# Cross attention by a product of the query weight and the memory keys: one change to a decoder step on one core

## The chip, the cores and the metric

The kernel runs on one core of a Trainium2 chip. The metric is the device time of one launch in microseconds (us). The core has five engines that run side by side and wait for each other through semaphores: TensorE (PE; its weight loads are shown as PEld), VectorE (DVE), ScalarE (ACT), GpSimd (POOL) and SyncE (SP). Sixteen DMA engines move data between HBM and the on-chip memory; transfers are issued from the queues of SP, ACT and POOL. Every engine executes its instructions in a fixed order. Before the change the median of three runs is 1817.83 us (1816.76 to 1819.05).

## The reference

One step of a decoder layer on two groups that share the weights: a prompt of 1024 rows of width 1024, and a sample group of 8 rows with long caches. Per layer: self-attention heads with a forget gate beside spatial gating heads, an output projection, then cross attention into 256 memory tokens, then a gated feed-forward network with a short convolution. The change concerns the cross attention of the prompt:

```python
def memory_kv(mem, g_mem, w_ck, w_cv):
    mn = rmsnorm(mem, g_mem)
    mk = (mn @ w_ck).reshape(B, M, MEM_HEADS, MEM_HEAD_DIM)     # 256 x 4 x 256, an output too
    mv = (mn @ w_cv).reshape(B, M, MEM_HEADS, MEM_HEAD_DIM)     # an output too

def cross_attend(xn, mk, mv, w_cq, w_co):
    q = (xn @ w_cq).reshape(B, T, MEM_HEADS, MEM_HEAD_DIM).astype(mk.dtype)
    s = jnp.einsum('bqhd,bmhd->bhqm', q, mk).astype(jnp.float32) * (MEM_HEAD_DIM ** -0.5)
    p = jax.nn.softmax(s, axis=-1).astype(mv.dtype)
    o = jnp.einsum('bhqm,bmhd->bqhd', p, mv).reshape(B, T, MEM_HEADS * MEM_HEAD_DIM)
    return (o @ w_co).astype(xn.dtype)
```

There are 4 heads of 256 columns, so queries, keys of all heads and values are each 1024 wide. All inputs are float32. The scores of a head are `xn @ (w_cq_h @ mk_h.T)`: the inner matrix does not depend on the rows.

## The kernel before

The prompt goes through in two halves of 512 rows. `prompt()` is a generator that chains the stages: `p1` (input projections of all rows), `attention(0)` (self-attention of the first half) mixed with a filler, `attention(1)`, and then for each half an output projection (`out_proj` with w_o), `cross`, which ends in `out_proj` with w_co, and `ffn`. The filler is `pmem()`, which computes the memory keys and values from `mem`, w_ck and w_cv, writes them to the outputs `o_mk` and `o_mv` and leaves them there to be read again, followed by the gating of the first half.

Every stage yields a planned time after each piece of work. Two planners use it. `mix(main, bg, ratio)` runs a filler beside a stage: it hands out filler worth `ratio` times the stage's planned time (`MIXR` for attention and `pmem`). And `build` itself runs the sample group beside everything: for each amount `PACE[phase]` of planned time it takes one step of the generator `sample()`. A step of its main part, `decode`, gathers one tile of 1 MB of cached keys (L1407), multiplies it by the query and reduces it on VectorE (L1423, L1427), and 18 steps later gathers the matching tile of values (L1469) and multiplies it on TensorE (L1475). `NKV` = 4 tiles (`kv`) are shared by these gathers. After 148 steps comes `sample_rest`, which is TensorE work on weights loaded once more. The final order on each engine is made by a scheduler from these instructions; a gather's place in the order hangs on the planned times.

Matmuls with weights are made of three products (`gemm3`, L272 to L274): each float32 operand is split into a high part of reduced precision (`h`, by a copy on ScalarE, L235 or L238) and a rest (`l`, by a subtraction on VectorE, L236 or L239), and high x high, high x low and low x high are accumulated. `wload` loads a weight tile of 128 x 1024 (512 KB) from the SP queue into one of `WR` = 4 buffers `wr` and splits it into `wh` and `wl`. The matmuls named fp32 below are made on unsplit float32 operands; the trace shows each of them as two instructions.

`norm_T` transposes the rows of a half 256 at a time, splits them with the gain and calls `first` when a group of 256 is there. `cross` before the change:

- loads keys and values of two heads (`fetch`), loads w_cq in two halves of 512 columns, and projects queries: for each of 8 blocks of 128 query columns, 24 products with 512 rows as the moving operand (`products`). The first block is computed in two groups of 256 rows from `norm_T`. The result is copied out of PSUM.
- `keys(h)`: four transposes bring a head's keys into place (L1153), a copy leaves PSUM (L1157).
- `weigh(h)`: for each of the four 128-row tiles two fp32 products of 256 columns (L1170), the maximum over two tiles on VectorE (L1172), the scaled exponentials (L1178) and the scaling by the reciprocal of the sum (L1183) on ScalarE.
- `turned(h)`: transposes of the weights (L1190) and their copy (L1191).
- `gather(h)`: the fp32 product with the values (L1198) and the split of the result for the output projection.

Other lines in the quoted rows: L640 the gating's mixing matmuls, L1106 the transposes in `norm_T`, L1055 to L1075 the matmuls of `out_proj`, L1545 the loads of `sample_rest`.

## Time and profile before

| | |
|---|---|
| median of three runs | 1817.83 us (1816.76 to 1819.05) |
| the profiled execution | 1820.56 us |
| its span, first to last instruction | 1818.4 us |
| mean granted TensorE clock | 0.986 |
| HBM traffic | 495.47 MB read, 23.93 MB written |
| DMA | 521.06 MB, mean 287 GB/s |

The page of the profile gives the busy time of each engine, 40 slices of the span, the DMA queues, the chain of work that ended last, and the costliest groups of instructions. A row of a group reads: line, engine, operation, written tile <- read tiles, shapes, count | busy time in us, mean length of one in ns | idle time of the engine just before, and what ended it. A row of a stretch reads: the stretch, its length, then per engine the busy time and the number of instructions, the granted clock, the share of time that the 16 DMA engines were busy, and GB/s. In the chain and in the timeline a row begins with the start in us from the span's start and the length.

By line numbers the stages stand as follows: `p1` up to 239 us, `attention(0)` with `pmem` and the first gating to about 349, `attention(1)` to 488, the first half's `out_proj` (w_o) to 548, `cross` without its output projection to 652, that projection to 707, `ffn` to 1107, the same for the second half to 1183, 1295, 1351 and 1818.

### The profile page before, as it was taken

What the parts mean: (1) busy time and instruction counts of PE and PEld (TensorE: products, weight loads), DVE (VectorE), ACT (ScalarE), POOL (GpSimd) and SP (SyncE); (2) the same over time, 40 slices, a digit from 0 to 9 for tenths busy, and PEclk for the clock granted to TensorE, in tenths of its full rate; (3) what the DMA queues carried; (4) which work ended last, traced back from release to release, by engine and by line L of the source; (5) the groups of instructions that cost most, each with busy time, mean ns of one, the idle gap of its engine ahead of it and who ended that gap; (6) DMA issues with size and microseconds to landing.
All of it is one profiled execution on the core that took longest, in us unless ns stands there. A gap on an engine that the chain in (4) does not pass through costs nothing.

```text
span 1818.4 us, 25090 instructions
## 1 busy us (share of the span) xinstructions
PE 1745.0 (96%) x9637; PEld 1294.9 (71%) x9637; DVE 1397.5 (77%) x1729; ACT 734.4 (40%) x1378; POOL 510.0 (28%) x461
## 2 busy tenths in 40 slices
PE   8999999888998999999999999989899999999997
PEld 5887776656676767777777776766576778767775
DVE  4689668888788877999989899898875549845344
ACT  6332365455643544433333244235353324332332
POOL 1252334332133432223332333334222111011110
PEclk9999999899999999999999999989999999999999
DMA  8886889777696986679878779988787777568982
GB/s 295 306 297 231 302 297 329 242 266 224 219 398 257 342 310 260 257 285 340 316 279 311 271 306 340 381 300 324 290 309 290 267 268 265 179 266 289 359 314 82
DMA packets 157074, 521.06 MB, mean 287 GB/s; under 512 B 20874, under 2 KB 40842, under 8 KB 124186
## 3 DMA queue, kind: packets, MB, share of 16 engines
q0 software_dynamic: 57168, 341.14, 49.5%
q1 hardware_dynamic: 92874, 165.73, 26.4%
q10 hardware_dynamic: 6912, 12.59, 1.8%
q8 instruction: 76, 1.25, 0.3%
q14 instruction: 44, 0.36, 0.1%
HBM read 495.47 MB, written 23.93 MB: 286 GB/s over the span
## 4 chain that ended last, share of the span: by engine, by line
PE 72%; DMA 10%; issue 7%; DVE 6%; ACT 2%; POOL 2%; SPq 0%; POOLq 0%; DVEq 0%; ACTq 0%
PE ba L272 11%; PE ba L274 11%; PE ba L273 11%; PE bb L272 5%; PE bb L273 5%; PE bb L274 5%; PE dv L1475 5%; DMA kv<-cache_k,io 3%; DMA wr<-w_in 2%; DMA kv<-cache_v,io 1%; PE dv L321 1%; PE dv L1751 1%; PE ba L1056 1%; PE ba L1055 1%; PE ba L1057 1%
## 5 line engine op out<-in xcount | busy, mean ns | idle before, releaser
L235 ACT ACTIVATE wh<-wr 128x1024 fp32r<-128x1024 f32 (+2 forms) x220 | 228.9, 1044 | 489.2 <-PE ba L273 156.0
L236 DVE TENSOR_TENSOR wl<-wr,wh 128x1024 fp32r<-128x1024 f32 (+2 forms) x220 | 262.5, 1200 | 175.6 <-PE ba L274 65.7
L1407 POOL DMA_INDIRECT kv<-cache_k,io x128 | 205.6, 1606 | 551.2 <-DVE s L1427 318.9
L1423 DVE TENSOR_TENSOR kv<-kv,d 128x1024 f32<-128x1024 f32 (+1 forms) x156 | 258.0, 1681 | 35.1 <-DMA kv<-cache_k,io 35.1
L1427 DVE TENSOR_REDUCE s<-kv 128x16 f32<-128x1024 f32 (+1 forms) x156 | 258.2, 1674 | 0.1
L1469 POOL DMA_INDIRECT kv<-cache_v,io x128 | 165.3, 1291 | 282.8 <-PE dv L1475 191.8
L272 PE MATMUL ba<-u,wh 128*128 128x512 f32 (+1 forms) x560 | 220.3, 395 | 1.7 <-ACT u L238 1.7
L273 PE MATMUL ba<-u,wh 128*128 128x512 f32 (+1 forms) x560 | 220.2, 393 | 1.7 <-DVE u L239 1.5
L274 PE MATMUL ba<-u,wl 128*128 128x512 f32 (+1 forms) x560 | 219.5, 393 | 0.0
L272 PE MATMUL ba<-wh,u 128*128 128x512 f32 (+1 forms) x495 | 186.9, 379 | 0.9 <-ACT u L235 0.9
L273 PE MATMUL ba<-wl,u 128*128 128x512 f32 (+1 forms) x495 | 185.4, 375 | 1.2 <-DVE wl L236 1.2
L274 PE MATMUL ba<-wh,u 128*128 128x512 f32 (+1 forms) x495 | 183.8, 376 | 0.0
L272 PEld LDWEIGHTS ba<-u,wh 128*128 128x128 f32 x560 | 106.8, 191 | 30.6 <-issue 5.6
L273 PE MATMUL bb<-u,wh 128*128 128x512 f32 (+1 forms) x304 | 119.4, 393 | 9.2 <-DVE u L239 9.2
L274 PEld LDWEIGHTS ba<-u,wl 128*128 128x128 f32 x560 | 106.9, 191 | 29.1 <-issue 6.1
L273 PEld LDWEIGHTS ba<-u,wh 128*128 128x128 f32 x560 | 106.7, 191 | 27.5 <-issue 2.7
L1475 PE MATMUL dv<-kv,s 128*32 128x512 f32 x1024 | 124.2, 598 | 1.8 <-DMA kv<-cache_v,io 1.8
L272 PE MATMUL bb<-u,wh 128*128 128x512 f32 (+1 forms) x304 | 119.4, 393 | 0.0
L274 PE MATMUL bb<-u,wl 128*128 128x512 f32 (+1 forms) x304 | 118.6, 390 | 0.0
L272 PEld LDWEIGHTS ba<-wh,u 128*128 128x128 f32 x495 | 93.0, 188 | 26.0 <-issue 6.9
L274 PEld LDWEIGHTS ba<-wh,u 128*128 128x128 f32 x495 | 92.8, 188 | 21.5 <-issue 3.7
L273 PEld LDWEIGHTS ba<-wl,u 128*128 128x128 f32 x495 | 93.1, 188 | 19.7 <-DVE wl L236 1.9
(425 smaller groups left out, 3255.9 us busy)
## 6 DMA issues: line engine op xcount, KB each, us to landing
wr<-w_up SPq DMA_DIRECT2D x88, 512.0 KB
kv<-w_up POOLq DMA_DIRECT2D x22, 1024.0 KB, 8.0
wr<-w_down SPq DMA_DIRECT2D x40, 512.0 KB
kv<-w_down POOLq DMA_DIRECT2D x11, 1024.0 KB, 8.5
wr<-w_in SPq DMA_DIRECT2D x16, 512.0 KB
wr<-w_o SPq DMA_DIRECT2D x16, 512.0 KB
wr<-w_cq SPq DMA_DIRECT2D x16, 512.0 KB
wr<-w_co SPq DMA_DIRECT2D x16, 512.0 KB
```

What stands on the lines that cost most here:

```text
L235: nc.scalar.activation(h, src, AF.Copy)
L236: nc.vector.tensor_tensor(l, src, h.bitcast(F32), op=ALU.subtract)
L272: mmul(out, sh, mh, start=(i == 0), stop=False)
L273: mmul(out, sh, ml, start=False, stop=False)
L274: mmul(out, sl, mh, start=False, stop=(i == n - 1))
L321: mmul(ps[32 * j : 32 * j + 32, :w], xT[:, k, :] if nk == 8 else xT[:, k * 8 : k * 8 + 32], raw[:, q, j * w : (j + 1) * w], start=(k == 0) ...
L1055: mmul(pss[i], mh[k][:, tb], wh, start=(k == korder[0]), stop=False)
L1407: nc.gpsimd.indirect_dma_start(kv, None, a["cache_k"], off(kidx[:, b, ch : ch + 1]))
L1423: nc.vector.tensor_tensor(kvv[:, i : i + m, :], kvv[:, i : i + m, :], qb.unsqueeze(1).broadcast_to((P, m, 512)), op=ALU.mult)
L1427: nc.vector.tensor_reduce(s[:, ch * 4 + i : ch * 4 + i + m, :].rearrange("p k h -> p (k h)"), kvv[:, i : i + m, :].rearrange("p k (h d) -> ...
L1469: nc.gpsimd.indirect_dma_start(kv, None, a["cache_v"], off(kidx[:, b, ch : ch + 1]))
L1475: mmul(dv[32 * j : 32 * j + 32, :], s[:, ch * 4 : ch * 4 + 4, :].rearrange("p k h -> p (k h)"), kvv[:, j, :], start=(ch == 1), stop=(ch == ...
```

## The change

The product of the query weight with the keys, `wk = w_cq_h @ mk_h.T` for all four heads (1024 x 1024), is made once, in `pmem`, and kept in HBM (`wk_d`). `cross` then takes the scores of two heads and 128 rows from one dense product of the normalised rows with `wk`, 512 columns wide, and does the softmax for each such tile.

- `pmem` first projects the keys, reads each half of them back (`fetched`), turns and splits them (`turned`: 8 transposes and 2 splits a half), then for each head and each half of the model's columns loads a tile of the transposed query weight (`w_cqT`, a new input prepared with the other layouts) and makes 12 products of 256 columns for each of two PSUM tiles, copies them out on ScalarE and writes them to `wk_d` from the ACT queue (`into_queries`). The values are projected after that.
- `cross` loads `wk_d` where it loaded w_cq. The rows are now the stationary operand (`scores`), and `norm_T` may get a generator from `first`, so that the first two row tiles are scored, and yield, when their rows are there. `weigh` takes one tile of 128 rows x 2 heads, `turned` transposes it four tiles later. The key loads, the key transposes and the fp32 scores are gone; the values are gathered as before.
- `out_proj` gets its left operand by a function `of(k, i)` and may run something after a k step (`between`): the last transposes and the gathers of heads 2 and 3 are run there.
- `MIXR` is 1.5 instead of 1.0.

```diff
-MIXR = 1.0
+MIXR = 1.5
...
+    wk_d = dram.tile([D, D], F32, tag="wk_d", name="wk_d")
...
+        def turned(t):
+
+            h2, l2 = U([P, 2, 512], F32R), U([P, 2, 512], F32R)
+            for j in range(2):
+                tr = TR()
+                for dd in range(2):
+                    for mt in range(2):
+                        nc.tensor.transpose(
+                            tr[:, dd * 256 + mt * P : dd * 256 + (mt + 1) * P],
+                            t[:, mt, j * 256 + dd * P : j * 256 + (dd + 1) * P],
+                            ident,
+                        )
+                split(tr, h2[:, j, :], l2[:, j, :])
+                yield 0.5
+            return h2, l2
+
+        def into_queries(n, h2, l2):
+
+            for j in range(2):
+                for c in range(2):
+                    w = wload(wpair(a["w_cqT"], n * 2 + j, c * 512, 512), 1024)
+                    for q in range(2):
+                        ps = MM()
+                        for i in range(2):
+                            mb = slice((q * 2 + i) * P, (q * 2 + i + 1) * P)
+                            gemm3(
+                                ps[:, i * 256 : (i + 1) * 256],
+                                [
+                                    (w[0][:, d_, mb], w[1][:, d_, mb], h2[:, j, d_ * 256 : d_ * 256 + 256], l2[:, j, d_ * 256 : d_ * 256 + 256])
+                                    for d_ in range(2)
+                                ],
+                            )
+                        t = T2()
+                        nc.scalar.activation(t, ps, AF.Copy)
+                        r0, c0 = c * 512 + q * 256, (n * 2 + j) * 256
+                        nc.scalar.dma_start(
+                            wk_d[r0 : r0 + 256, c0 : c0 + 256].rearrange("(a p) k -> p a k", p=P), t.rearrange("p (a k) -> p a k", k=256)
+                        )
+                    yield 2.9
+
+        raws = []
+        for n in range(2):
+            yield from project(a["w_ck"], mk_d, n)
+            raws.append(fetched(mk_d, n))
+        for n in range(2):
+            h2, l2 = yield from turned(raws[n])
+            yield from into_queries(n, h2, l2)
+        for n in range(2):
+            yield from project(a["w_cv"], mv_d, n)
...
     def cross(xt, sq):
...
+        loaded = lambda n: [wload(wpair(wk_d, kk, n * 512, 512), 1024) for kk in range(4)]
...
+        def scores(i, hs, ls):
+            ps, tb = MM(), slice(i * P, (i + 1) * P)
+            gemm3(
+                ps,
+                [(hs[k][:, tb], ls[k][:, tb], ws[k // 2][0][:, k % 2, :], ws[k // 2][1][:, k % 2, :]) for k in range(8)],
+            )
+            return ps
+
+        def weigh(n, i, ps):
+
+            sv = ps.rearrange("p (j m) -> p j m", m=256)
+            mx, bs, l, r = (sm([P, 2], tag, 2) for tag in ("cmx", "cbs", "cl", "cr"))
+            nc.vector.tensor_reduce(mx, sv, axis=AX.X, op=ALU.max, negate=True)
+            nc.scalar.activation(bs, mx, AF.Copy, scale=rq[:, i : i + 1])
+            pp = T2().rearrange("p (j m) -> p j m", m=256)
+            for j in range(2):
+                nc.scalar.activation(
+                    pp[:, j, :], sv[:, j, :], AF.Exp, bias=bs[:, j : j + 1], scale=rq[:, i : i + 1], accum_out=l[:, j : j + 1]
+                )
+            nc.vector.reciprocal(r, l)
+            for j in range(2):
+                nc.scalar.activation(pp[:, j, :], pp[:, j, :], AF.Copy, scale=r[:, j : j + 1])
+            weights.append((n, i, pp))
...
+        def first(hs, ls, c):
+            i0 = c.start // P
+            r = rows_rstd(sq, i0, i0 + 2)
+            nc.vector.tensor_scalar(rq[:, i0 : i0 + 2], r, 1.0 / 16, None, op0=ALU.mult)
+            for i in (i0, i0 + 1):
+                weigh(0, i, scores(i, hs, ls))
                 yield 5.2
...
+        hs, ls = yield from norm_T(xt, G_CROSS, first)
+        ws = loaded(1)
+        for i in range(4):
+            ps = scores(i, hs, ls)
+            turned()
+            weigh(1, i, ps)
+            yield 5.6
+            if i == 1:
+                fetch(0)
+                fetch(1)
+        turned()
+        for h in range(2):
+            gather(h)
+            turned()
+            fetch(h + 2)
+            yield 3.8
...
+        yield from out_proj(a["w_co"], of, xt, ys=ys, between={0: turned, 1: partial(gather, 2), 2: partial(gather, 3)})
```

195 lines of the change are left out of this document (61 added, 134 removed).

## The prediction

> **What bounds the kernel now.** I read the page first, then the busy table by stretches, then single groups in the two stretches that the change rewrites, then start times of neighbouring matmuls. The page:
>
> ```profile
> span 1818.4 us, 25090 instructions
> PE 1745.0 (96%) x9637; PEld 1294.9 (71%) x9637; DVE 1397.5 (77%) x1729; ACT 734.4 (40%) x1378; POOL 510.0 (28%) x461
> PE 72%; DMA 10%; issue 7%; DVE 6%; ACT 2%; POOL 2%; SPq 0%; POOLq 0%; DVEq 0%; ACTq 0%
> ```
>
> TensorE is busy nearly all the time and carries 72% of the chain that ended last, so what counts is TensorE work and the holes in it. The stretches that matter (length; then busy time and instructions of PE, PEld, DVE, ACT, POOL; granted clock; DMA share; GB/s):
>
> ```profile
> 239.00:349.00 110.00, 101.77 (x550) 77.57 (x549) 83.61 (x144) 61.18 (x131) 40.81 (x52) 0.99 0.84 302
> 548.00:652.00 104.00, 97.36 (x502) 69.52 (x500) 88.00 (x114) 53.18 (x125) 37.52 (x25) 0.97 0.85 318
> 1183.00:1295.00 112.00, 98.67 (x499) 69.30 (x499) 95.00 (x113) 52.72 (x122) 41.71 (x29) 0.94 0.83 306
> 1351.00:1380.00 29.00, 27.38 (x165) 21.01 (x164) 17.84 (x32) 17.80 (x38) 4.09 (x6) 0.94 0.49 193
> 1380.00:1410.00 30.00, 30.00 (x160) 19.10 (x159) 14.64 (x21) 9.70 (x17) 7.36 (x8) 1.00 0.94 344
> 1410.00:1440.00 30.00, 30.00 (x152) 20.07 (x152) 16.19 (x23) 10.82 (x18) 5.72 (x7) 1.00 0.95 348
> ```
>
> 239 to 349 is the first half's self-attention with the memory projections as filler; 548 to 652 and 1183 to 1295 are the two halves' cross attention up to its output projection; from 1351 on stands the second half's FFN. The cross stretches are the ones where TensorE falls short of the stretch and the clock dips.
>
> A busy matmul is not its cost, since matmuls overlap. Cost per matmul is the distance between starts: first and last of 29 products with 260 columns, then of 21 with 512.
>
> ```profile
> 83.79 0.28 PE L272 MATMUL ba<-wh,u 128*128 128x260 f32 x1
> ...
> 87.16 0.28 PE L273 MATMUL bb<-wl,u 128*128 128x260 f32 x1
> ...
> 299.64 0.39 PE L272 MATMUL bb<-wh,u 128*128 128x512 f32 x1
> ...
> 304.24 0.40 PE L274 MATMUL bb<-wh,u 128*128 128x512 f32 x1
> ```
>
> 3.37 us over 28 steps is 0.120 us, 4.60 over 20 is 0.230.
>
> Now both cross stretches together (216 us), by source line in this order: L1170 fp32 scores, L1153 key transposes, L1198 value gather, L1475 decode's value products, L1190 and L1106 transposes, L640 gating.
>
> ```profile
> sum 216.00, PE 32.07 PEld 24.65; mean PE 16.03 PEld 12.33
> sum 216.00, PE 5.00 PEld 3.97; mean PE 2.50 PEld 1.98
> sum 216.00, PE 24.47 PEld 10.15; mean PE 12.23 PEld 5.07
> sum 216.00, PE 25.01 PEld 5.42; mean PE 12.51 PEld 2.71
> sum 216.00, PE 8.57 PEld 7.26; mean PE 4.28 PEld 3.63
> sum 216.00, PE 8.80 PEld 6.96; mean PE 4.40 PEld 3.48
> sum 216.00, PE 2.21 PEld 2.17; mean PE 1.11 PEld 1.08
> ```
>
> These give 106.1 us. The query projection is 168 products of 512 columns and 48 of 256 per half: 336 x 0.230 + 96 x 0.120 = 88.8. Together 194.9; the other 21.1 us of the two stretches are stalls. Which:
>
> ```profile
> L273 PE MATMUL bb<-u,wh 128*128 128x256 f32 x16 | 5.8, 362 | 3.2 <-DVE u L239 3.2
> L1170 PE MATMUL ba<-t,u 128*128 128x256 f32 x40 | 9.6, 387 | 0.7 <-ACT t L1157 0.7
> L273 PE MATMUL bb<-u,wh 128*128 128x256 f32 x16 | 6.0, 376 | 6.0 <-DVE u L239 6.0
> L1170 PE MATMUL ba<-t,u 128*128 128x256 f32 x56 | 13.2, 384 | 1.9 <-ACT t L1157 1.9
> L1170 PE MATMUL bb<-t,u 128*128 128x256 f32 x8 | 3.6, 636 | 4.2 <-DVE u L236 4.2
> ```
>
> The first two rows are of the first half, the others of the second: 9.2 us wait for VectorE's split of the normalised rows (L239), 6.8 us stand before the fp32 scores. Named: 16.0 us.
>
> **The change, term by term.**
>
> *TensorE work.* Removed in both halves: scores and key transposes, 32.07 + 5.00 = 37.1 us. The projection by w_cq becomes the product with wk_d: 192 products of 512 columns a half, 2 x 192 x 0.230 = 88.3 for 88.8, nothing. Softmax transposes and gather keep their counts. Added once, in pmem: 192 products of 256 columns x 0.120 (nearest row: 260 columns) = 23.0, and 16 transposes at 5.00/32 = 0.16, 2.5. TensorE is full around them, so both lie on the path. Net 25.5 - 37.1 = -11.6 us.
>
> *Stalls in cross.* In after, each k step of the first stage has two tiles of 512 columns (6 x 0.230 = 1.4 us) behind each split where before had 3 x 0.120 = 0.36, so L239's 9.2 us can go; the scores with their 6.8 us are gone. In their place comes a longer softmax chain per tile (maximum, two exponentials, reciprocal, two scalings, transposes), which the order covers by the four next score tiles, 22 us. Bounds: 16.0 gained to 0 (other waits replace them). Decode still holds VectorE for 88 and 95 us of these stretches, so I take half: -8.
>
> *The attention stretch (239 to 349).* It gets the 25.5 us of TensorE work, and on the queues: SP issues eight w_cqT loads and two read-backs of the memory keys, ACT sixteen writes of wk_d. Two things can be late. First, the read-back: the key write and the read must land before the transposes, and attention's matmuls queue behind these on TensorE.
>
> ```profile
> kv<-cache_k,io POOLq DMA_INDIRECT x128, 8.5
> q1 hardware_dynamic: 92874, 165.73, 26.4%
> ```
>
> With 8.5 us each (the nearest landing) 17.0 are needed; the next column half's two tiles cover 48 x 0.230 = 11.0, attention's steps between them more. So 0 to 6.0. Second, traffic: 4 MB read, 4 MB written, 1 MB read back, and two decode steps that by the yields and PACE fall into this stretch (10 instead of 8), 2 MB each: 13 MB, at 302 GB/s 43 us. Free are 0.16 x 110 = 17.6 plus 25.5 of new length, 43.1: an even match. The writes go in 1 KB pieces; at q1's mean packet (0.264 x 1818.4 x 16 / 92874 = 0.083 us) 4096 of them take 21 us of all engines, where 4 MB at 302 GB/s take 13, so 8 may stick out. Bounds 0 to 14, I take 4: the read-back is the nearer case, and part of its cover is certain.
>
> *VectorE and ScalarE there.* Eight weight splits, four key splits, two decode steps:
>
> ```profile
> L236 DVE TENSOR_TENSOR wl<-wr,wh 128x1024 fp32r<-128x1024 f32 x208 | 252.3, 1219 | 154.5 <-PE ba L274 65.7 <-issue 25.1 <-PE bb L274 16.4
> L1427 DVE TENSOR_REDUCE s<-kv 128x32 f32<-128x2048 f32 x68 | 154.1, 2274 | 0.1
> ```
>
> 8 x 1.22 + 4 x 0.6 (half the columns) + 2 x 2 x 2.27 (a step's product taken as long as its reduction) = 21.2 us on VectorE, which has 26 us free before the stretch is lengthened: hidden. ScalarE has 49 us free for the same splits, sixteen copies out of PSUM and sixteen issues: hidden. If this cover were gone, the splits that feed the new products would add their 12 us.
>
> *Edits at nothing.* The reads of wk_d take the place of those of w_cq on the same queue, with the same size and the same splits. SP loses eight 256 KB loads of keys. Passing `of` instead of lists issues nothing; `between` moves the last softmax transposes and two heads' gathers among the output projection's matmuls, where they cost what they cost before, and covers their own chain. MIXR 1.5 hands out the longer filler faster, so that it still ends with attention.
>
> *Decode displaced.* Cross yields 20 units of planned time less per half at the same PACE. Following the yields: 19 steps for 21 in the first half's middle, 22 for 25 in the second's, two more in attention, and 22 instead of 18 left when the second FFN begins; the last key steps now fall there. That is 4 value and 2 key tiles of 1 MB: 6 MB at 348 GB/s, 17 us. The DMA engines are free for 0.51 x 29 + 0.06 x 60 = 18 us there: 0 to 17. If the slots (NKV = 4) fill late, what is late next is VectorE's key products and, queued behind them, the splits that the FFN's matmuls wait for. I take 4. Sample's last product comes nearer to the end, but the prompt's still ends last.
>
> *Sum.* -11.6 - 8 + 4 + 4 = -11.6 us. The span of 1818.4 becomes 1806.8. The profiled execution took 1820.56, 2.2 outside its span; the median of the runs is 1817.83, 2.7 below that execution, so in its terms I expect 1806.2, say 1806 us.
>
> **Rivals.**
>
> *Slower: decode moves instead of shrinking.* Place: cross and the front of the second FFN. For it speak two links of the chain of waits within the second cross stretch:
>
> ```profile
> 1226.57 10.73 DMA kv<-cache_k,io
> 1261.66 13.70 DMA kv<-cache_k,io
> ```
>
> There key gathers, not matmuls, hold the chain. Then no stall goes, and the displaced 6 MB cost their whole 17 us: -11.6 + 0 + 4 + 17 = +9.4, 1827 us. It decides as soon as the FFN's front costs over 7.6 us with no stall gained. Against it: DMA is at 0.49 just there.
>
> *Less gain: the attention stretch.* Read-back and small writes cost their whole 14: -11.6 - 8 + 14 + 4 = -1.6, 1816 us. For it the even balance of traffic, against it the many steps of attention between.
>
> *More gain.* All 16.0 us of stalls go and nothing new comes: -27.6, 1790 us.
>
> *Weight loads bound.* Each new product loads its own weights. If loads, not starts, add up, the removed loads are 24.65 + 3.97 = 28.6 us and the added 192 x 0.189 + 16 x 0.124 = 38.3:
>
> ```profile
> L272 PEld LDWEIGHTS ba<-wh,u 128*128 128x128 f32 x74 | 14.0, 189 | 0.0
> 66.00:109.00 43.00, 43.00 (x355) 42.15 (x353) 43.00 (x29) 12.48 (x22) 15.66 (x8) 1.00 0.77 275
> ```
>
> So +9.7 in place of -11.6, 1828 us with the other terms as taken. The last row speaks against it: 353 loads in 42.15 us are 0.119 each, though one lasts 0.189; they overlap too. The Trainium skill, "Perfetto Trace Analysis", section "Identifying the Most-Contended Engine", has this as a rule: matmul busy time is a bad measure of headroom, the summed time of weight loads a good one. By that rule the change adds TensorE load; by the row, loads at this shape can be summed to more than the wall.
>
> **How the numbers follow.** Chances: my forecast 0.45 (own range 1798 to 1814), more gain 0.09, decode moved 0.22, attention stretch 0.18, loads 0.06. A change of 0.2% (3.6 us) is about what a measurement of this kernel tells from none. Faster: 0.45 + 0.09 + 0.10 of the attention case = 0.64; same: 0.05 of it; slower: 0.22 + 0.06 + its last 0.03 = 0.31. The range goes from the full gain, 1790, to the slower cases with a few more us of the attention stretch's 14, 1832.
>
> **What the profile after would show.** Right: fp32 matmuls of 256 columns gone; 192 of 256 columns in attention starting 0.12 us apart; the two cross stretches together some 167 us instead of 216 (37 of work, 8 of stalls, five decode steps at 25.01/26); attention some 30 us longer. Wrong: matmuls waiting for a DMA of o_mk or for VectorE behind key gathers at the FFN's front, cross stretches together above 175 us, or 0.19 us between the new products.

## The result and the profile after

The changed kernel takes 1837.99 us in the median of five runs (1832.35 to 1841.27), the kernel before 1817.83 beside it (1815.47 to 1822.79): ratio 1.0101, 95% interval 1.0076 to 1.0127. It is about 1% slower, where 1806 was forecast. The profiled execution took 1834.17 us; of its page:

```profile
PE 1744.2 (95%) x9637; PEld 1290.1 (70%) x9637; DVE 1411.0 (77%) x1755; ACT 746.5 (41%) x1386; POOL 496.0 (27%) x463
PE 63%; DVE 9%; DMA 3%; issue 2%; ACT 2%; POOL 1%; DVEq 0%; POOLq 0%; ACTq 0%
```

TensorE is busy as long as before (1745.0 us), though by the prediction's count it has 11.6 us less to do, and its share of the chain that ended last falls from 72 to 63%, VectorE's rises from 6 to 9%. Busy time is time, not work: the granted clock is lower, as the view by cores has it after and before,

```profile
core 0: 1832.4 us, clock 0.980
```
```profile
core 0: 1818.4 us, clock 0.986
```

The mean covers idle time too. Counted by the clock records of the traces over TensorE's busy time alone, 53.4 us stood at half the clock after and 41.0 before, so 6.2 us were lost in this way, over half of the work saved. TensorE's holes, the span less its busy time, grew from 73.4 to 88.2 us, about as much as the span, which is 14.0 us longer. (By the medians the loss is 20.2; the profiled execution is among the changed kernel's shorter ones.) Where, the busy table by stages tells (columns as before); the kernel before first: attention, the first FFN, and the second FFN in two parts.

```profile
239.00:497.00 258.00, 231.17 (x1435) 167.22 (x1434) 206.04 (x359) 153.37 (x335) 86.97 (x114) 0.97 0.75 257
707.00:1135.00 428.00, 422.16 (x2013) 314.98 (x2012) 394.63 (x382) 162.31 (x264) 127.78 (x89) 0.99 0.80 300
1351.00:1391.00 40.00, 38.38 (x220) 28.67 (x219) 23.98 (x41) 22.03 (x45) 6.78 (x8) 0.96 0.61 228
1391.00:1818.00 427.00, 417.16 (x2760) 311.11 (x2758) 242.71 (x363) 135.52 (x242) 64.96 (x93) 1.00 0.71 259
```

and the kernel after: attention; cross attention and its output projection; the first FFN; the second cross attention and its projection; the front of the second FFN and its rest.

```profile
239.00:538.00 299.00, 264.70 (x1670) 195.52 (x1669) 231.22 (x387) 176.75 (x370) 92.06 (x116) 0.95 0.76 267
587.00:660.00 73.00, 66.33 (x329) 47.40 (x328) 57.84 (x86) 41.26 (x104) 18.58 (x15) 0.98 0.69 257
660.00:724.00 64.00, 63.95 (x300) 43.59 (x299) 57.80 (x66) 21.03 (x40) 22.49 (x17) 1.00 0.90 345
724.00:1160.00 436.00, 427.09 (x2041) 319.18 (x2040) 405.07 (x394) 163.57 (x266) 132.58 (x94) 0.98 0.80 300
1207.00:1285.00 78.00, 71.56 (x353) 48.18 (x350) 63.25 (x89) 42.67 (x102) 20.86 (x19) 0.98 0.75 280
1285.00:1344.00 59.00, 59.00 (x271) 41.19 (x268) 54.08 (x57) 20.42 (x39) 23.48 (x18) 1.00 0.87 337
1344.00:1384.00 40.00, 31.12 (x170) 23.64 (x168) 31.40 (x39) 17.79 (x36) 13.55 (x10) 0.87 0.69 267
1384.00:1832.00 448.00, 434.40 (x2856) 319.19 (x2855) 259.25 (x385) 146.71 (x256) 75.23 (x103) 0.99 0.73 270
```

The next table has the stages of every run in us, from one profiled execution each. Attention is counted from 239 us to the first matmul of the w_o projection; the cross stages, with their output projection w_co, and the FFNs are cut at the first transpose of each `norm_T` and the first matmul of the second w_o projection. The two w_o projections stand between these columns. The expectations quoted below count attention only to its own last work, 249 us before and 287 after. The ratio is to the kernel before, with its 95% interval.

| run | ratio | attention | cross, w_co 1 | FFN 1 | cross, w_co 2 | FFN 2 |
|---|---|---|---|---|---|---|
| before | 1 | 258.1 | 159.1 | 428.6 | 168.2 | 467.6 |
| after | 1.0101 (1.0076 to 1.0127) | 298.8 | 137.6 | 436.1 | 136.4 | 488.9 |
| keys_only | 1.0205 (1.0163 to 1.0246) | 298.6 | 161.6 | 427.3 | 162.9 | 463.1 |
| unwritten | 1.0051 (1.0033 to 1.0069) | 293.7 | 138.3 | 436.6 | 136.7 | 487.7 |
| slots | 1.0080 (1.0059 to 1.0101) | 298.8 | 137.7 | 437.6 | 128.1 | 490.0 |
| pace | 1.0118 (1.0092 to 1.0144) | 302.5 | 137.7 | 449.2 | 138.3 | 477.4 |
| thin_before | 0.9286 (0.9270 to 0.9301) | 235.5 | 150.3 | 387.1 | 136.3 | 449.5 |
| thin_after | 0.9081 (0.9062 to 0.9100) | 256.1 | 116.7 | 386.1 | 115.1 | 450.0 |
| gate | 1.0087 (1.0064 to 1.0111) | 300.5 | 141.7 | 439.2 | 136.1 | 486.5 |
| hold | 1.0047 (1.0032 to 1.0062) | 302.0 | 135.4 | 435.1 | 128.5 | 489.5 |
| hold_slots | 1.0070 (1.0048 to 1.0091) | 301.2 | 135.0 | 433.8 | 128.6 | 488.6 |
| hs_att | 1.0153 (1.0136 to 1.0170) | 298.8 | 131.9 | 442.7 | 129.5 | 498.7 |
| hs_ffn | 1.0151 (1.0122 to 1.0179) | 301.1 | 135.6 | 453.3 | 136.6 | 478.9 |
| hs_mix1 | 1.0133 (1.0116 to 1.0150) | 300.0 | 133.6 | 439.8 | 129.4 | 502.9 |
| after_light | 1.0153 (1.0119 to 1.0186) | 296.6 | 133.1 | 433.7 | 134.1 | 507.5 |
| before_light | 1.0108 (1.0083 to 1.0132) | 256.3 | 163.1 | 426.5 | 165.8 | 474.7 |
| hs_light | 1.0182 (1.0160 to 1.0205) | 299.2 | 129.8 | 434.0 | 135.4 | 514.9 |
| hs_light2 | 1.0155 (1.0128 to 1.0181) | 286.5 | 129.1 | 426.7 | 137.9 | 516.9 |
| hs_mid1a | 1.0066 (1.0041 to 1.0090) | 304.2 | 135.4 | 432.8 | 131.1 | 491.9 |
| hs_mid1b | 1.0060 (1.0035 to 1.0086) | 302.7 | 135.2 | 434.0 | 131.4 | 495.1 |

Five of these runs (`after`, `keys_only`, `pace`, `gate`, `hold`) have the same order of instructions in attention on every computing engine, but for a few missing records, and five others (`slots`, `hold_slots`, `hs_ffn`, `hs_mid1a`, `hs_mid1b`) share another. The first five took 298.6 to 302.5 us there, the others 298.8 to 304.2: a difference under some 5 us in attention, read from one execution each, tells little. In the second FFN, `after`, `slots` and `unwritten`, nearly the same in order, lie within 2.3 us.

From before to after: attention +40.7, the cross stages -53.3, the FFNs +28.8, the two w_o projections -2.2; together the span's +14.0. Part of it is decode that changed places. Its value products (L1475 before, L1497 after) in the two cross stages and in the two FFNs, before:

```profile
sum 327.00, PE 38.69 PEld 8.24; mean PE 19.34 PEld 4.12
sum 895.00, PE 57.71 PEld 12.52; mean PE 28.86 PEld 6.26
```

and after:

```profile
sum 274.00, PE 30.52 PEld 6.42; mean PE 15.26 PEld 3.21
sum 924.00, PE 64.95 PEld 14.19; mean PE 32.48 PEld 7.09
```

So, with the prediction's figures for the work, the cross stages lost 37.1 of work, 8.2 of moved products and 8.0 of stalls. The FFNs gained 7.2 of moved products and 21.6 of something else, attention 25.5 of work, 1.9 of two more decode steps and 13.3 of something else. The two remainders, 34.9 us, are what the experiments are about. They are nearly all holes and low clock: TensorE's holes grew from 26.8 to 34.3 us in attention and from 17.3 to 31.4 in the FFNs, and its busy time at half the clock by 8.2 and 13.0 us, half of which is lost; that is 11.6 of the 13.3 and 20.6 of the 21.6. Key steps of the decode, counted as reduced tiles (L1427 before, L1449 after): cross stages 17 and 20 before, 13 and 15 after; FFNs 41 and 0 before, 43.5 and 5 after.

The largest single place is the second FFN's front. In 20 us TensorE is busy 12.75 after, 18.38 before:

```profile
1344.00:1364.00 20.00, 12.75 (x75) 9.85 (x73) 17.20 (x23) 10.29 (x24) 9.84 (x6) 0.74 0.76 301
```
```profile
1351.00:1371.00 20.00, 18.38 (x120) 15.21 (x118) 11.30 (x22) 13.40 (x31) 1.30 (x3) 0.91 0.32 124
```

What TensorE waits for there most (waits, us in total, times, longest), and the timelines of ScalarE, GpSimd, VectorE and again ScalarE at that moment, of the changed kernel:

```profile
PE ba L1164 <- ACT u L1092: 4.1, 1, 4.1
PE bb L274 <- DVE u L240: 2.4, 2, 1.6
```
```profile
1347.40 0.29 ACT L1079 ACTIVATE fac<-sqx,part 128x1 f32<-128x1 f32 x1
```
```profile
1347.95 1.73 POOL L1429 DMA_INDIRECT kv<-cache_k,io  x1 [5.50 <-PE dv L1497]
1349.99 0.94 POOL L1491 DMA_INDIRECT kv<-cache_v,io  x1 [0.30 <-issue]
1350.96 2.77 POOL L1080 TENSOR_TENSOR fac<-fac,mhalf 128x1 f32<-128x1 f32 x1
```
```profile
1350.96 2.35 DVE L1445 TENSOR_TENSOR kv<-kv,d 128x1024 f32<-128x1024 f32 x2
```
```profile
1353.76 1.33 ACT L1092 ACTIVATE u<-u,fac 128x512 f32<-128x512 f32 x2 [4.16 <-POOL fac L1080]
```

The row factor scales a row tile for the FFN (L1080 makes it, L1092 uses it). ScalarE has its input ready at 1347.69. Two gathers of the decode stand ahead of the factor on GpSimd until 1350.93, and the factor itself lasts 2.77 us, to 0.42 us after VectorE has multiplied a gathered key tile; ScalarE waits 4.16 us for it and TensorE's transposes for ScalarE. Before, no key step was left when this FFN began; after, five were.

Two more places are of this kind. At the first FFN's transposes TensorE waits 4.1 us for VectorE's gating product, which stands behind a key tile's two products (2.35 us):

```profile
PE bb L1164 <- DVE u L651: 4.1, 1, 4.1
```

And in the middle of the second FFN, at 1576 us, it waits 4.4 us for the FFN's own convolution on VectorE, which stands behind the sample group's cross attention (L1679, L1681):

```profile
L273 PE MATMUL ba<-wh,u 128*128 128x512 f32 (+1 forms) x578 | 220.4, 384 | 4.4 <-DVE t L1309 4.4
```

`slots`, `unwritten` and `gate` have this last wait with 4.3 to 4.4 us, `hold` and `hold_slots` one of 6.8 and 6.9 there; the kernel before and `keys_only` have no wait over 2.5 us in either FFN.

### The profile page after: what moved, and what is told of

The parts are those of the page before. It is cut to its first block, busy times and chain, and to the rows that moved or that the text cites. A ratio compares the mean times of both kernels' runs of the same rounds, so it can differ in the third digit from the quotient of the medians.

```text
span 1832.4 us, 25200 instructions
## 1 busy us (share of the span) xinstructions
PE 1744.2 (95%) x9637; PEld 1290.1 (70%) x9637; DVE 1411.0 (77%) x1755; ACT 746.5 (41%) x1386; POOL 496.0 (27%) x463
## 4 chain that ended last, share of the span: by engine, by line
PE 63%; DVE 9%; DMA 3%; issue 2%; ACT 2%; POOL 1%; DVEq 0%; POOLq 0%; ACTq 0%
PE ba L275 9%; PE ba L274 9%; PE ba L273 9%; PE dv L1497 5%; PE bb L275 5%; PE bb L273 5%; PE bb L274 5%; DVE kv L1445 1%; DVE s L1449 1%; PE dv L322 1%; PE dv L1773 1%; DMA kv<-cache_v,io 1%; PE ba L1131 1%; PE ba L1133 1%; PE ba L1132 1%
## 5 line engine op out<-in xcount | busy, mean ns | idle before, releaser
L1429 POOL DMA_INDIRECT kv<-cache_k,io x128 | 174.0, 1359 | 601.7 <-DVE s L1449 364.2
L1449 DVE TENSOR_REDUCE s<-kv 128x16 f32<-128x1024 f32 (+1 forms) x152 | 255.4, 1698 | 0.0
L273 PE MATMUL ba<-wh,u 128*128 128x512 f32 (+1 forms) x578 | 220.4, 384 | 4.4 <-DVE t L1309 4.4
L274 PE MATMUL ba<-wl,u 128*128 128x512 f32 (+1 forms) x578 | 219.8, 382 | 1.2 <-DVE wl L237 1.2
L275 PE MATMUL ba<-wh,u 128*128 128x512 f32 (+1 forms) x578 | 217.7, 382 | 1.8 <-DVE u L237 1.8
L274 PE MATMUL ba<-u,wh 128*128 128x512 f32 (+1 forms) x512 | 198.4, 388 | 0.9 <-DVE u L240 0.9
L273 PE MATMUL ba<-u,wh 128*128 128x512 f32 (+1 forms) x512 | 197.5, 387 | 0.6 <-ACT u L239 0.6
L275 PE MATMUL ba<-u,wl 128*128 128x512 f32 (+1 forms) x512 | 197.2, 386 | 0.0
L273 PEld LDWEIGHTS ba<-wh,u 128*128 128x128 f32 x578 | 109.5, 190 | 36.2 <-issue 10.4
L1497 PE MATMUL dv<-kv,s 128*32 128x512 f32 x1024 | 128.0, 610 | 6.6 <-DMA kv<-cache_v,io 6.6
L275 PEld LDWEIGHTS ba<-wh,u 128*128 128x128 f32 x578 | 109.7, 190 | 28.6 <-issue 5.9
L274 PEld LDWEIGHTS ba<-wl,u 128*128 128x128 f32 x578 | 109.5, 189 | 26.5 <-DVE wl L237 3.5
L274 PEld LDWEIGHTS ba<-u,wh 128*128 128x128 f32 x512 | 97.3, 190 | 31.1 <-issue 11.5
L273 PEld LDWEIGHTS ba<-u,wh 128*128 128x128 f32 x512 | 97.4, 191 | 24.3 <-issue 4.0
L275 PE MATMUL bb<-wh,u 128*128 128x512 f32 (+1 forms) x286 | 109.8, 384 | 4.5 <-DVE u L240 4.5
L273 PE MATMUL bb<-wh,u 128*128 128x512 f32 (+1 forms) x286 | 110.0, 385 | 1.5 <-ACT t L1216 1.5
L274 PE MATMUL bb<-wl,u 128*128 128x512 f32 (+1 forms) x286 | 108.7, 380 | 0.8 <-DVE wl L237 0.8
```

Source lines behind the costliest of these rows:

```text
L273: mmul(out, sh, mh, start=(i == 0), stop=False)
L274: mmul(out, sh, ml, start=False, stop=False)
L275: mmul(out, sl, mh, start=False, stop=(i == n - 1))
L1429: nc.gpsimd.indirect_dma_start(kv, None, a["cache_k"], off(kidx[:, b, ch : ch + 1]))
L1449: nc.vector.tensor_reduce(s[:, ch * 4 + i : ch * 4 + i + m, :].rearrange("p k h -> p (k h)"), kvv[:, i : i + m, :].rearrange("p k (h d) -> ...
L1497: mmul(dv[32 * j : 32 * j + 32, :], s[:, ch * 4 : ch * 4 + 4, :].rearrange("p k h -> p (k h)"), kvv[:, j, :], start=(ch == 1), stop=(ch == ...
```

## The experiments

The theories, by the letters that the expectations use. A: decode steps moved to the second FFN's front make the loss, and the planner's count of steps can undo it. B: the attention stretch alone makes it, by ScalarE's order (B1) or by full DMA engines (B2, D where the decode's gathers are the other half of the traffic). C: it is TensorE work and its clock. E: the change gains by itself, and its meeting with the decode, wherever that is, turns the gain. F: VectorE and late gathers are the limit in the first FFN.

**The making of the matrix alone** (`keys_only`). To the kernel before:

```diff
-MIXR = 1.0
+MIXR = 1.5
+    wk_d = dram.tile([D, D], F32, tag="wk_d", name="wk_d")
     (pmem as in the changed kernel; cross as before)
```

> The kernel before with only the making of the matrix added (the changed order in the memory projections, the transposes, the products, the writes, and the ratio 1.5); cross attention is as before and nothing reads the matrix. Its decode begins the second feed-forward at step 131, no later than before. Theory B: attention goes from 249 to about 287 us and nothing is given back, 1818 + 38 = about 1856, ratio 1.021. Theory C (only the counted work of 25.5 us is added, and the rest of the 38 comes from elsewhere): about 1843, ratio 1.014. The difference between this run and the changed kernel is what cross attention itself gave, with the displaced decode: 37.1 us of products alone would leave the changed kernel at 1819, so what is missing from that is theory A's share.

Measured 1849.84 us, +33.6. Attention is 298.6 long, as in the changed kernel; the FFNs are no longer than before (427.3 and 463.1). So the whole of attention's loss is in the making, and the FFNs' loss belongs to the new cross attention: against this run the changed kernel wins 50.5 us in the cross stages and gives 34.6 of them back in the FFNs. The new cross attention alone, without the making, was not tried.

**The planner's prices in the cross stages** (`pace`).

```diff
-PACE = {... 'mid0': 8.0, ... 'mid1': 6.8, ...}
+PACE = {... 'mid0': 7.4, ... 'mid1': 6.1, ...}
```

> The changed kernel with only the planner's prices for a decode step lowered in the two stages that hold cross attention (8.0 to 7.4 and 6.8 to 6.1), so that the second feed-forward begins at decode step 129 of 147 as it did before the change, not at 125. Theory A (decode steps pushed into the second feed-forward's front, where their last key gathers and the row factor's power stand in one queue, turn the gain into a loss): the second feed-forward goes from 488 back to about 470 us, the two cross stretches grow by some 2 us each for the steps that they take back, and the kernel takes about 1823 us, ratio 1.003. Theory B (the attention stretch alone costs it, 38 us longer for 25.5 us of work): the second feed-forward gives back only the displaced steps themselves, which the cross stretches take, and the kernel stays near 1837, ratio 1.010.

1839.74 us. The second FFN did shrink by 11.5, but the first grew by 13.1, and there TensorE now stands for values that have not landed:

```profile
PE dv L1497 <- DMA kv<-cache_v,io: 9.5, 4, 4.1
```

Also, of the four steps that the plan put ahead of the second FFN, key work of only 2.5 went there: 2.5 of 5 key tiles still fell behind its start. Theory A in its simple form, that putting the plan's count right undoes the loss, fell.

**The writes' tiles, and no writes** (`slots`, `unwritten`).

Both diffs are shortened.

```diff
-                        t = T2()
-                        nc.scalar.activation(t, ps, AF.Copy)
+                    t = U([P, 2, 512])                      # once for both q
+                        nc.scalar.activation(t[:, q, :], ps, AF.Copy)
```
```diff
-                        nc.scalar.dma_start(wk_d[...], t...)
...
-        loaded = lambda n: [wload(wpair(wk_d, kk, n * 512, 512), 1024) for kk in range(4)]
+        loaded = lambda n: [wload(wpair(a["w_cq"], kk, n * 512, 512), 1024) for kk in range(4)]
```

> The changed kernel with only the tiles changed from which the new matrix is written out: eight pairs of large tiles in place of sixteen of the seven half-kilobyte-column slots that the attention's own tiles share. Theory B1 (ScalarE stands in order behind slots that a write has not yet left): its waits of 1.7 to 4.1 us on those writes go, and the attention stretch falls from 287 to about 278 us, the kernel to about 1829, ratio 1.006. Theory B2 (the DMA engines are full: share 0.91 to 1.04 from 289 to 364 us, at 342 to 383 GB/s, for 9 MB more to move): the writes land no sooner, the wait moves to weight tiles, and the stretch stays within 3 us of 287. Theory A expects no change outside noise either.

> The changed kernel without the sixteen writes of the new matrix (4 MB): its products and copies are made and dropped, and cross attention reads the query weights at the matrix's place, same sizes and same number of loads, so its scores are those of another product. Theory B (writes hold slots and fill the DMA engines): the attention stretch falls from 287 to about 276 us, the kernel to about 1827, ratio 1.005. Theory C (it is TensorE work and its clock): the stretch falls by under 3 us, 1836, ratio 1.010. Theory A expects the second feed-forward at 488 as in the changed kernel either way.

With the large tiles attention does not move (298.8): B1 fell. That run's lower median, 1830.46, comes from a place nobody had named, the second cross stretch, where TensorE's instructions stand in another order though the edit is in attention; its interval overlaps the changed kernel's. Without the writes attention is 5.1 us shorter, half of what theory B had expected, or up to 9 against the other runs with attention's order, and the FFNs stay long. So the writes cost 5 to 9 us of attention's excess.

**The same pair with a thin decode** (`thin_before`, `thin_after`). Both kernels leave out seven eighths of the decode's gathers with their work on VectorE and TensorE:

```diff
             qb, s = st
+            if ch % 8:
+                nc.vector.memset(s[:, ch * 4 : ch * 4 + 4, :], 0.0)
+                (the same yields)
             kv = KV()
...
             s = st[1]
+            if ch not in (1, 14):
+                return lambda after=None: None
             kv = KV()
```

> The kernel before with seven eighths of the decode's cache steps left out: of the 16 chunks of each sequence only two are gathered, multiplied and reduced for the keys and only two for the values, and the scores of the others are set to zero, so the sampled rows' attention is another sum. The planner's order and counts are as before. TensorE loses 112 value steps of 0.96 us, about 108 us, VectorE some 112 x 4.7 us: about 1700 us. It is the partner of the next run.

> The changed kernel with the same seven eighths of the decode's cache steps left out. Theory E (the change by itself gains; what turns it into a loss is its meeting with the decode: steps that lose their cover and stand ahead of the feed-forward's first splits and row factors on VectorE and GpSimd): it comes out 5 to 15 us faster than the thinned kernel before, 25.5 us of work and some 6 us of writes against 37.1 us of products and 5 us of stalls in cross attention. Theory B (the attention stretch alone eats the gain, by transfers and ScalarE's order): 0 to 12 us slower than its partner, attention again about 40 us longer.

1688.58 and 1651.96 us: here the change gains 36.6 us, ratio 0.978 (0.9081 / 0.9286; 0.975 to 0.981 from both intervals). With the whole decode it loses 20. Attention grows by 20.6 instead of 40.7, the FFNs by -0.5 instead of 28.8, and the cross stages fall by 54.8. Cross attention with its projection, thin_before and then thin_after:

```profile
520.00:670.00 150.00, 139.10 (x637) 107.96 (x636) 68.82 (x119) 68.99 (x154) 7.35 (x8) 0.97 0.33 112
1102.00:1238.00 136.00, 130.25 (x608) 100.76 (x607) 57.78 (x81) 69.35 (x152) 6.79 (x7) 1.00 0.29 102
```
```profile
540.00:656.00 116.00, 115.62 (x528) 88.50 (x526) 63.23 (x114) 61.37 (x143) 6.47 (x7) 1.00 0.41 144
1087.00:1202.00 115.00, 113.09 (x503) 85.47 (x502) 60.68 (x88) 61.83 (x139) 7.38 (x8) 1.00 0.35 122
```

TensorE's holes, 16.7 us in the first pair of rows (lengths less busy time), are 2.3 in the second: with the thin decode the new order has hardly a stall. Theory E is borne out and theory B is not enough: more than half of what the decode takes away lies outside attention. Which of the decode's parts does it, its transfers, its VectorE work or its place in the queues, the pair cannot tell, since all were thinned together. In attention the decode's part shows too: 25.5 us of added TensorE work lengthen it by 20.6 us where the decode is thin and by 40.7 where it is whole. The stretch where the new matrix is made: first the changed kernel, with TensorE's and ScalarE's longest wait in it, then thin_after with TensorE's.

```profile
289.00:314.00 25.00, 18.16 (x126) 14.57 (x125) 21.38 (x33) 11.99 (x21) 11.26 (x10) 0.86 0.91 342
314.00:339.00 25.00, 20.15 (x151) 15.53 (x151) 17.49 (x30) 13.09 (x30) 3.74 (x5) 0.93 1.00 367
```
```profile
PE bb L919 <- ACT t L908: 6.8, 1, 6.8
```
```profile
ACT wh L236 <- DMA wr<-w_cqT: 5.1, 1, 5.1
```
```profile
284.00:309.00 25.00, 22.35 (x185) 19.89 (x184) 15.51 (x22) 17.36 (x35) 1.80 (x4) 1.00 0.91 293
309.00:334.00 25.00, 25.00 (x167) 21.53 (x167) 14.66 (x25) 16.88 (x34) 4.69 (x9) 1.00 0.88 277
```
```profile
PE bb L919 <- ACT t L908: 1.2, 1, 1.2
```

With the whole decode's gathers beside them, the tiles of the transposed query weight come late: the one that ScalarE stands for was issued at 289.11 us and split at 298.81, in thin_after the same tile was issued at 281.35 and split at 285.0. Attention's copy (L908) stands behind that split on ScalarE and TensorE behind the copy. `unwritten` has the same wait of TensorE with 7.6 us, so the writes do not make it. Full DMA engines alone are not the difference either: their share is 0.91 and 0.88 in thin_after.

**Two edits at the FFN's entry** (`gate`, `hold`).

```diff
-                ys = yield from mix(cross(xt, sq), gating(1), 0.05)
+                ys = yield from mix(cross(xt, sq), gating(1), 0.06)
```
```diff
-                held[0] = len(group) == 2
+                held[0] = len(group) == 2 or ys is not None
```

> The changed kernel with one number changed: the gating of the second half of rows is mixed into cross attention at 0.06 instead of 0.05 of its planned time, so that its last steps, which now stand at the first feed-forward's entry because cross attention became shorter, are issued inside cross attention as they were before the change. If that remainder is what TensorE waits for there (4.2 us before the first transposes, ended by VectorE's gating product, in the changed kernel, 6.2 us with the planner's prices lowered), the kernel takes about 1833 us, ratio 1.008; if the wait only changes its name to the next VectorE work in the queue, 1838.

> The changed kernel with the decode held back earlier: no decode step is issued from the first row tile of the output projection's second half in cross attention until the feed-forward's entry is through (before, only from its last two row tiles). Theory E: VectorE and GpSimd come to the entry without key steps ahead of the row factors and splits; the holes of 6.7 and 9.3 us at the two entries shrink to about 3 each, two steps more move behind the entry (2 us), and the kernel takes about 1830 us, ratio 1.007. Theory B expects 1838.

`gate`, 1835.41 us, cannot be told from the changed kernel. TensorE's wait for the gating at the first FFN's transposes got another name, and a new one came inside cross attention:

```profile
PE bb L1197 <- DMA t<-o_mv: 4.0, 1, 4.0
PE bb L1164 <- ACT u L1092: 3.7, 1, 3.7
```

`hold` took 1826.51 us, 11.5 less than the changed kernel (by the ratios, each to the kernel before in the same session, 9.8; their intervals do not overlap), but not where expected: the second FFN stays at 489.5 (its first wait falls from 4.1 to 2.6), while the second cross stretch goes from 136.4 to 128.5. There one wait had cost 4.5 us, in the changed kernel

```profile
PE bb L275 <- DVE u L240: 4.5, 1, 4.5
```

and in `hold` 0.2. The figure of the forecast was met by another cause than the one that it named.

**Edits on top of hold and slots.** `hold_slots` has both; each of the next three adds one number:

```diff
-PACE = {'p1': 7.0, 'att0': 12.0, ... 'att1': 11.0, ...}
+PACE = {'p1': 7.0, 'att0': 24.0, ... 'att1': 7.5, ...}      # hs_att
-... 'ffn0': 8.5 ...
+... 'ffn0': 7.9 ...                                          # hs_ffn
-MIXR = 1.5
+MIXR = 1.0                                                   # hs_mix1
```

> The two edits that helped alone, together: the new matrix written out of large tiles, and the decode held back from the first row tile of cross attention's output projection. Each alone took about 8 us out of the second cross stretch. If they removed the same wait (TensorE standing 4.7 us for VectorE's second split there, with the lower clock after it), the pair gives 1826, as the hold alone; if the slots free ScalarE in attention as well, 1820 or less.

> As the run with both edits, and in attention's first half the planner's price of a decode step is doubled (12 to 24), in its second half lowered (11 to 7.5): four steps of 2 MB each leave the stretch in which the new matrix is made, and three of them are taken up 100 us later. Theory D (the attention stretch is 13 us longer than its added TensorE work because 9 MB more transfers meet the decode's gathers there; the thinned pair added only 20.6 us): attention falls from about 300 to about 290 us. Theory B1 (ScalarE's order, whatever the gathers do): attention stays at 298 or more. The rest: one step more behind, +1 us.

> As the run with both edits, and the planner's price of a decode step in the first feed-forward lowered from 8.5 to 7.9, so that three steps more are done there and the second feed-forward begins at step 126, not 123. Theory A: three steps of 0.96 us and the key steps at the entry leave the second feed-forward, which falls by 8 us or more, and the first grows by 3: about 5 us in all. Theory F (VectorE is the limit in the first feed-forward, 92 to 100 of a hundred busy, and gathers come late when more are asked for, as in the run with the lowered prices in cross attention, where value steps waited 10 us for them): the first feed-forward grows by 8 us or more and nothing is won.

> As the run with both edits, and the memory projections and the new matrix are mixed into attention at the old ratio 1.0, not 1.5: the same transfers and products spread over 149 planned us instead of 100. Theory D: fewer transfers per us beside the gathers, attention falls by 3 to 8 us, unless what remains at the end of the first half runs uncovered, which adds up to 10. Theory C (it is work and its order): within 3 us of the run with both edits.

The two edits took out the same wait, 1826.24 us together. Each further number made it about 15 us slower: 1842.82, 1842.19, 1841.03. `hs_ffn` fits theory F: three steps more cost the first FFN 19.5 us and spare the second 9.7; TensorE's longest waits in the first are for VectorE and for gathers:

```profile
PE ms L1482 <- DVE dg L1475: 7.2, 1, 7.2
PE dv L1497 <- DMA kv<-cache_v,io: 6.3, 4, 1.9
```

`hs_att` made the last exponential of attention's first half 18 us earlier (at 400 us for 418), and the second half, with the steps moved there, gave most of it back (123 for 110). `hs_mix1` left attention as it was, within 1.2 us; theory D's version of the mixing fell.

**Fewer steps in attention, with and without the change** (`after_light`, `before_light`, `hs_light`, `hs_light2`).

```diff
-PACE = {'p1': 7.0, 'att0': 12.0, 'attx': 26.0, ...}
+PACE = {'p1': 7.0, 'att0': 24.0, 'attx': 26.0, ...}      # the first three
+PACE = {'p1': 7.0, 'att0': 40.0, 'attx': 40.0, ...}      # hs_light2
```

> The changed kernel with the planner's price of a decode step doubled (12 to 24) in attention's first half alone: four key steps fewer there, three or four more at the second feed-forward's start (121 instead of 125). Theory D (the matrix's transfers and the decode's gathers fill the DMA engines together): attention falls from 299 to about 283 us, the second feed-forward grows by four steps of 0.96 us and their key work, 5 to 10 us: about 1828 us, ratio 1.006. If a step costs the same wherever it stands: 1836 or more.

> The kernel before with the same single edit. If the price of steps in attention's first half is the matrix's (theory D), this one wins little there, 4 us, and pays the same behind: 1816 to 1822. If steps there are as dear without the matrix, it gains 10 us: about 1806, and the comparison of the change has to be made against that.

> The changed kernel with the large tiles for the writes, the decode held back earlier at the feed-forward's entry, and the doubled price in attention's first half. If the parts add up: 1826 - 18 + 7 = about 1815, level with the kernel before; if the entry to the second feed-forward, which now meets four key steps more, gives it back: 1828.

> As the run before it, with the price in attention's first half at 40 in both of its parts, so that only two steps fall into it and the second feed-forward begins at step 118. Theory D: attention falls by another 3 to 6 us, the second feed-forward grows by 2 to 4 and the sampled rows' last work ends within 10 us of the end: 1810 to 1818. If attention has no contention left to lose, it is slower than the run before it by 2 us.

None was faster than what it started from: 1842.87, 1833.83, 1849.22 and 1841.75 us. Fewer steps do shorten attention where enough of them leave, by 14.7 us in `hs_light2` against `hold_slots`, but ten key tiles then fall into the second FFN for five, and it grows by 28.3. The telling one is `before_light`: the kernel before, with no operation changed and one planner's number doubled, loses 20 us (1.0108), as much as the change does. Its profiled execution, the shortest of its four, shows 9.9 of them: the second FFN +7.1, the w_o projections +5.0 and the first cross stage +4.0, with the other stages 6.2 shorter together. In both kernels the first half of attention ends sooner (364 for 377 us, 400 for 420) and the second half, from there to its own last exponential, takes 13 us longer in the old kernel (123 for 110) and 17 in the changed one (123 for 106), though no more key tiles are reduced in it (7.75 both times, and 7.5 for 7.75); why, no run here shows.

**More steps in the second cross stretch** (`hs_mid1a`, `hs_mid1b`).

```diff
-'mid1': 6.8
+'mid1': 5.2      # hs_mid1a; 5.6 in hs_mid1b
```

> The changed kernel with the large tiles, the decode held back earlier, and the price of a decode step in the second cross stretch lowered from 6.8 to 5.2, so that the second feed-forward begins at step 129 as before the change and attention, the first cross stretch and the first feed-forward are as in the run with the two edits. If the steps at the entry are the loss: the second feed-forward falls from 489 to about 472, the cross stretch takes 6 us more, and the kernel takes 1815, level with before. If the second cross stretch's VectorE and gathers are as full as the first feed-forward's, it pays it back there: 1826 or more.

> The same at 5.6: step 127 at the second feed-forward's start. Between the two: 1818 to 1822 if the entry is the loss; 1826 or more if not.

1831.73 and 1827.86 us, no gain. The plan had the second FFN begin at step 129 and 127 instead of 123, but the work did not follow: counted from the trace, VectorE reduced 15.5 key tiles in that cross stage in both, 15 in `hold_slots`, 15 in the changed kernel, 20 in the kernel before, and 4.5 (for 5) remained behind the FFN's start. A key step takes 131 / 15.5 = 8.5 us there, 136.4 / 15 = 9.1 in the changed kernel and 168.2 / 20 = 8.4 in the kernel before; neither lower price put a step more into the stage. In the first cross stage it is longer, 159.1 / 17 = 9.4 before and 137.6 / 13 = 10.6 after. What holds a step is, as the waits over the whole span suggest, partly its buffer: the groups of gathers on GpSimd, before and then after, with the idle time in front of them and what ended it:

```profile
L1407 POOL DMA_INDIRECT kv<-cache_k,io x128 | 205.6, 1606 | 551.2 <-DVE s L1427 318.9 <-PE dv L1475 129.4 <-DMA kv<-x 23.1
```
```profile
L1429 POOL DMA_INDIRECT kv<-cache_k,io x128 | 174.0, 1359 | 601.7 <-DVE s L1449 364.2 <-PE dv L1497 97.4 <-DVE s L1437 59.1
```

Most of that idle time ends when VectorE's reduction or TensorE's value product gives one of the four tiles back. Whether more tiles would help was not tried.

No version here beats the kernel before; `hold` is the nearest, 0.47% slower.

## Why the prediction was wrong

The stage sums against the terms on record:

| term | predicted | measured |
|---|---|---|
| TensorE work | -11.6 | not measured as a sum; the new products start 0.12 us apart |
| Stalls in cross | -8 (0 to -16) | -8.0 (thin pair: -54.8 in all, so -17.7) |
| The attention stretch | +4 (0 to 14) | +13.3 (to 17 by the other runs with its order) |
| Decode displaced | +4 (0 to 17), at one place | +21.6 in both FFNs |
| w_o projections, moved products | 0 | -2.2, +0.9 |

The excess, 9.3 + 17.6 - 2.2 + 0.9 = 25.6 us, is the distance between the forecast span, 1806.8, and 1832.4.

**TensorE work** held as far as the runs show it. In attention's timeline the starts of eleven neighbouring products, the first and the last shown, span 1.20 us, 0.12 each:

```profile
313.57 0.28 PE L273 MATMUL ba<-u,wh 128*128 128x256 f32 x1
...
314.77 0.28 PE L274 MATMUL ba<-u,wh 128*128 128x256 f32 x1
```

With that the rival of the weight loads is gone, and the rule of the Trainium skill beside it, "Perfetto Trace Analysis", section "Identifying the Most-Contended Engine", did not decide here: the busy time of the loads fell from 1294.9 to 1290.1 us, and their times added up rose by 2.8 us, from 1596.0 to 1598.8, not by the 9.7 of the rival.

**Stalls in cross** held in size, and in its mechanism only in part. In the first cross stage TensorE's holes are as long as before, 6.7 for 6.6 us: the waits named in the prediction went, and one value product waited 5.1 us for its gather instead. In the second stage they fell from 13.3 to 6.4, and 4.5 of what is left is a wait for the split of the normalised rows (L240, before L239), which was to go. That the half taken for safety was met to the figure is luck. The thin pair shows that nearly all stalls go where the decode is thin.

**The attention stretch** had the right suspects and too small a sum: 13.3 is just inside its bound of 14. The traffic was called an even match; in fact the DMA engines are at 0.91 to 1.00 for 50 us, and 5 to 9 us are the writes. No engine waits for the read-back; only the SP queue stands in front of its two loads, 7.4 us in all. One way in which the rest arrives was not on the list: through ScalarE's order, a weight tile in front of attention's copies.

**Decode displaced** is the step that failed. It saw which steps would move, 4 value and 2 key tiles at the second FFN, and priced them as transfers that find the DMA engines free. The engines were not full (0.69 over that front's 40 us); what was full were the queues in front of the critical work: GpSimd with gathers ahead of the row factor, VectorE with key tiles ahead of the splits. It did name key products queued ahead of the FFN's splits, but took only 4 us for them. And it looked at one place, while the first FFN, with 43.5 key steps for 41, lost 7.5 us too, 1.9 of them moved products; there a key tile stood ahead of the gating on VectorE. Of the prediction's own signs of being wrong one came true: at the second FFN's front TensorE waits behind key gathers and key products. The rival "decode moves instead of shrinking", 1827 us, had the direction, and its place in the second FFN; but it let the cross stages win no stall, and they won 8. So neither was the case: the cross stages gained what was forecast, and the decode took more than that back elsewhere.

Behind it stands a reading error in the first part of the prediction. "What counts is TensorE work and the holes in it" is true of the kernel as it was, with the decode's steps under it. But a key step had its own time of 8.4 to 9.4 us in the cross stages, with VectorE at 85% there, and stages that end 53 us sooner take fewer of them along: 13 + 15 key steps for 17 + 20. The trace had shown both, the key gathers in the chain of waits and VectorE's 88 and 95 us. They were used for a rival's chance of 0.22 and to halve the stalls, but the price of the steps that were left over was not raised by them.

What stays open: how much of the FFNs' 21.6 us is the lost cover, and how much a planner whose numbers no longer fit the order. `before_light` shows that moving three key steps out of attention cost the old kernel 20 us as well; that no edit of the changed kernel that keeps its result gave more than some 12 back does not show that none would. Taking the row factor off GpSimd, or putting it ahead of the gathers, was not tried.

## What to carry to other kernels

When work runs in the background of a stage, price a change of the stage twice, with the background and without: a pair of runs with the background thinned told in one comparison what the others only circled (-36.6 us with the thin background, +20 with the whole). A stage that is made shorter carries less of the background along, and the rest lands where nothing was prepared for it; look at the queues of the engines there, not only at whether the DMA engines are free. And where constants have been fitted to an order of work, move one of them in the old kernel before blaming the new one.

## What the runs showed of the hardware

A 128 x 1 power on GpSimd takes 0.56 us alone. In the front of the second FFN it took 2.77 us and ended at 1353.73, just after VectorE's two key products, which had started with it and ended at 1353.31; in the kernel before:

```profile
1353.29 0.56 POOL L1024 TENSOR_TENSOR fac<-fac,mhalf 128x1 f32<-128x1 f32 x1 [3.70 <-ACT fac L1023]
```

The twenty traces hold 160 of these powers. For 45 a VectorE operation on two SBUF tiles (TENSOR_TENSOR) was running when they began, with over 0.1 us to go, or began in the same instant, and every one of them ended 0.41 to 0.44 us after the end of such an instruction. The other 115 took 0.54 to 0.59 us, also those beside a VectorE reduction or an instruction with one input in PSUM. The Trainium skill, "SBUF — State Buffer", section "Who interferes with whom", has the rule: a VectorE instruction with both inputs in SBUF contends with a GpSimd instruction that reads SBUF, and the port pair that they share is an exclusive lock. The 160 rows agree with it.

A hole costs more than its length. The wait of 4.1 us at the second FFN's front ends at 1354.54. Half the clock stands from 1351.70, within the wait, to 1361.9, over 7 us beyond its end, as the granted clock of this row shows (third figure from the end):

```profile
1351.70:1361.90 10.20, 6.26 (x26) 5.73 (x27) 7.40 (x10) 5.86 (x13) 5.18 (x4) 0.50 0.75 312
```

In it five neighbouring products, the first and the last shown, start 0.21 us apart instead of 0.12:

```profile
1357.02 0.41 PE L275 MATMUL bb<-u,wl 128*128 128x256 f32 x1
...
1357.87 0.41 PE L273 MATMUL bb<-u,wh 128*128 128x256 f32 x1
```

In the clock records of `before` and `after` such stretches last 3.41, 6.83 or 10.24 us, one, two or three times 3.41, save the last one of each run. The Trainium skill, "TensorE: Matmul & The Clock Gate", section "What's actually happening", tells of a clock that drops to half after an idle window of about 3.4 us and needs a busy one to return; the stretches agree with that length.
